# Adaptive-norm parameters from transposed weights on VectorE, half a block at a time

## The chip, the cores and the metric

One core of a Trainium2 chip. The metric is the device time in microseconds of one execution; the time before is the median of three runs. TensorE (PE) does the matrix products, PEld is its weight load, VectorE (DVE), ScalarE (ACT) and GpSimd (POOL) the elementwise work, SyncE (SP) issues most loads.

## The reference, cut to what matters

Two layers of a trunk over 512 tokens of width 1024, with 256 context tokens. Layer 0 mixes by attention, layer 1 by a convolution module; behind each stands an expert mixer with product keys. Every sub-layer is modulated by parameters that come from the conditioning vector `c` alone:

```python
def ada_params(cond, w, b):
    return jnp.split(jax.nn.silu(cond) @ w + b, 6, axis=-1)
...
for l in range(DEPTH):
    sh1, sc1, g1, sh2, sc2, g2 = ada_params(c, w_ada[l], b_ada[l])     # w_ada[l]: 1024 x 6144
    a_lat = modulate(rms_norm(h_lat, g_norm1[l]), sh1, sc1)            # x * (1 + scale) + shift
    ...
    h_lat = h_lat + g1[:, None, :] * y_lat
    h_lat = h_lat + g2[:, None, :] * peer_ffn(modulate(rms_norm(h_lat, g_norm2[l]), sh2, sc2), *peer_p)
```

For each layer that is one vector of 1024 times a matrix of 1024 x 6144. In `peer_ffn` each token has 8 heads with 2 key halves; from 128 keys of each half the best 16 are taken, and the best 16 of their sums name the experts whose rows of two tables (16384 x 1024) act on the token.

## The kernel before

The 6144 columns of a layer's parameters are cut into 48 blocks of 128: blocks 0 to 7 are sh1, 8 to 15 sc1, 16 to 23 g1, 24 to 31 sh2, 32 to 39 sc2, 40 to 47 g2. Shifts and scales are wanted as columns (one parameter on each partition, `par`, [128, 48]), the two gates as rows on all partitions (read back from a [128, 1024] tensor in DRAM, `g1d` and `g2d`). A block of weights is [128, 8, 128], 512 KB in pieces of 512 bytes. Each stage computes the blocks in its own way:

- Start: blocks 0 to 15 of layer 0 are products on PE (L985).
- Projections of the attention (span 41 to 235 us): layer 0's blocks 16 to 23, by a `stepper` with method "v". Eight products with a column of the conditioning vector are added up on DVE (L752, L754), a ones-matmul on PE sums over the partitions (`bcast`, L893) and DVE adds the bias (L894).
- Attention (235 to 505 us): layer 0's blocks 24 to 39, method "g". POOL does products and sums (L765 to L768), PE transposes the result (L886), DVE sums it (L888) and adds the bias (L889).
- Front of the first mixer: layer 1's blocks 6 to 19 on PE (`on_pe`: a gate by L807, a column by L805, 8 products each), one in each of the 16 head halves and a second in the first two. The loop over the halves (`hp`) multiplies the tokens with 512 KB of query weights in three passes (L142 to L144), copies the result on ACT and scores it against the keys (L257); DVE takes the best 16 (`top16`, L215; L219 is its maximum). DVE and ACT then prepare the first expert rows (u_hi L169, u_lo L173).
- Side step of the first mixer: layer 1's blocks 20 to 23 on PE (L807) while the gate matrix is built (`gbuild`).
- First expert loop: layer 0's blocks 40 to 47 and layer 1's 0 to 5 and 24 to 39, 30 blocks, by `slow`, three iterations for a block. DVE adds up four products in the first, four in the second (L852, L854); in the third PE does the ones-matmul (L869, L872) into PSUM columns that the scores leave free, and the next block's load is issued into the one buffer. DVE adds the bias an iteration later.
- Front of the second mixer: layer 1's blocks 40 to 47 on PE (L807), in the first half of the head halves.

The expert loop goes over 128 chunks of 128 experts. An iteration scores a chunk of `u` (three passes, `s1`), loads a later chunk of `v` (`load_v`, L558) and of `u` (L164), splits the next `v` into a high and a low part (`prep`: v_hi on ACT L579, v_lo on DVE L581), accumulates on PE (`s2`, L602, 18 products) and does two or three steps of the fourth token tile, whose experts' rows are gathered one by one (`fetch` on POOL L613, `gather_step` on DVE L621, L625). For the first 97 iterations `u` and the ada step are part of it.

Engines take their instructions in the order in which the code emits them, and that order is written out by hand; a load on SP's queue waits for its buffer, and what is emitted later on SP waits behind it. The lines of the loop that set it:

```python
    for m in range(NCHUNK):
        ...
        load_v(m + 4 if tail else m + 2 if m + 2 < busy else m + 3)
        while pdone < min(m + 1 + tail, NCHUNK - 1):
            pdone += 1
            prep(pdone, c + 1 if c + 1 < NCHUNK else None)
        ...
        while gdone < goal:
            gather_step(gdone)
            gdone += 1
        if beside is not None and c < NCHUNK:
            try:
                beside.send(room)
```

Of the kernel before, what the change touches and what calls it, by code (L numbers as in the profile page):

```python
# [23 lines left out]
D = 1024  # L24
KD = 8
# [14 lines left out]
B0, B1, B2, B3, FRONT_TWICE = 8, 6, 20, 40, (0, 1)  # L40

# [3 lines left out]
HOW = "vga"  # L45
# [101 lines left out]
def peer(k, h, xr, h_done, A, sh, g2d, wq, sk, uT, un, vn, out_open, out_cb, side=None, front=None, slow=None):  # L147
# [116 lines left out]
    front_step = front and front(qp, lambda: psf.tile([128, TT, 128], F32, name="gp", bufs=4))  # L264
    for hp in range(16):
# [47 lines left out]
    while front_step is not None and front_step():  # L313
        pass
# [164 lines left out]
    side_step = side and side(gp, lambda: psf.tile([128, TT, 128], F32, name="scp", bufs=2))  # L479

# [32 lines left out]
    for b in range(nb):  # L513
# [15 lines left out]
        if side_step is not None:  # L529
            side_step()  # L530
    while side_step is not None and side_step():
        pass
# [126 lines left out]
    beside = slow(bs) if slow is not None else None  # L659
    if beside is not None:  # L660
        next(beside)
# [4 lines left out]
    for m in range(NCHUNK):  # L666
# [8 lines left out]
        if c < NCHUNK:  # L675
            room = s1p[c][:, NTD:T]
            s1_gelu(c)
# [22 lines left out]
        if beside is not None and c < NCHUNK:  # L700
            try:
                beside.send(room)
            except StopIteration:
                beside = None
        if m == busy:
            nc.sync.dma_start(hres, hd)
            nc.sync.dma_start(hg, g2d)
# [26 lines left out]
class Ada:  # L734
# [3 lines left out]
    def __init__(self, k, l, cond, w, bT, brow):  # L738
        self.k, self.l, self.cond, self.w, self.bT, self.brow = k, l, cond, w, bT, brow
        self.par = k.const.tile([128, 48], F32, name="ada_par%d" % l)  # L740

    def load(self, pool, f0, bufs):
        t = pool.tile([128, KD, 128], F32, name="ada_w", bufs=bufs)
        self.k.nc.sync.dma_start(t, self.w[:, f0:f0 + 128].rearrange("(kk p) f -> p kk f", p=128))
        return t

    def partial(self, how, t, acc):

        nc = self.k.nc
        c = self.cond  # L750
        if how == "v":
            nc.vector.tensor_scalar(acc, t[:, 0, :], c[:, 0:1], None, op0=OP.mult)  # L752
            for kk in range(1, KD):
                nc.vector.scalar_tensor_tensor(acc, t[:, kk, :], c[:, kk:kk + 1], acc, op0=OP.mult, op1=OP.add)  # L754
            return
        g = nc.gpsimd
        for kk in range(KD):
            if how == "a" or (how == "m" and kk % 2):
                nc.scalar.activation(t[:, kk, :], t[:, kk, :], AF.Copy, scale=c[:, kk:kk + 1])
        if how == "m":  # L760
            t2 = t.rearrange("p (k two) f -> p k two f", two=2)[:, :, 0, :]
            g.tensor_tensor(t2, t2, c.rearrange("p (k two) -> p k two", two=2)[:, :, 0:1].to_broadcast([128, 4, 128]),
                            op=OP.mult)
        if how == "g":
            g.tensor_tensor(t, t, c[:, :, None].to_broadcast([128, KD, 128]), op=OP.mult)  # L765
        g.tensor_tensor(t[:, 0:4, :], t[:, 0:4, :], t[:, 4:8, :], op=OP.add)
        g.tensor_tensor(t[:, 0:2, :], t[:, 0:2, :], t[:, 2:4, :], op=OP.add)
        g.tensor_tensor(acc, t[:, 0, :], t[:, 1, :], op=OP.add)  # L768

    def stepper(self, pool, psum, blocks, eng, g1_dst, g2_dst, lag=1, wbufs=2):  # L770

        nc = self.k.nc
        todo, loaded, accs, stores = list(blocks), [], [], []

        def reduce(f, acc):
            p = psum()
            if f // 8 in (2, 5):
                o = f % 8 * 128
                br = pool.tile([128, 128], F32, name="ada_br", bufs=lag)
                nc.sync.dma_start(br, row_bcast(self.brow[f * 128:(f + 1) * 128], 128))  # L780
                self.bcast(p[:, 0, :], acc[:, 0, :], br, br)
                stores.append(((g1_dst if f < 24 else g2_dst)[:, o:o + 128], br))
            else:
                self.columns(p, acc, f, 1)

        summed = []

        def on_pe():

            if stores:  # L790
                nc.sync.dma_start(*stores.pop(0))
            if summed:
                f, p, br = summed.pop(0)
                if br is None:
                    nc.vector.tensor_tensor(self.par[:, f:f + 1], p[:, 0, 0:1], self.bT[:, f:f + 1], op=OP.add)
                else:
                    nc.vector.tensor_tensor(br, p[:, 0, :], br, op=OP.add)
                    o = f % 8 * 128
                    stores.append(((g1_dst if f < 24 else g2_dst)[:, o:o + 128], br))
# [17 lines left out]
        if eng == "p":  # L817
            return on_pe
# [17 lines left out]
    def slow(self, pool, blocks, dst=None):  # L836
# [20 lines left out]
        for n, f in enumerate(blocks):  # L857
            acc = pool.tile([128, 128], F32, name="ada_acc", bufs=2)
            if after:
                after.pop(0)()  # L860
# [1166 lines left out]
```

## Time and profile before

| | us |
|---|---|
| median of 3 runs | 3362.16 (3361.88 to 3362.23) |
| profiled execution, its own time | 3360.77 |
| its span | 3359.0 |
| PE busy | 3206.8 (95%) |
| DVE busy | 2578.6 (77%) |
| ACT busy | 1283.1 (38%) |
| POOL busy | 1009.9 (30%) |

The span is the time from the first to the last instruction of one profiled execution. Busy times of an engine are sums over its instructions. The chain of waits goes back from the last instruction, at each step to what released it. A row of the chain or of a timeline has its start and its length in us; x counts the instructions in it, and brackets hold the idle time before it and what ended that.

### The profile page before, as it was taken

The numbers are of one execution on the slowest core, as the hardware profiler recorded it, in microseconds if no ns is written. First come the engines' busy times: TensorE is split into PE (matmuls) and PEld (weight loads), VectorE is DVE, ScalarE is ACT, GpSimd is POOL, SyncE is SP. The second block draws the span as 40 slices with busy tenths as digits, with TensorE's granted clock in tenths as the row PEclk, the third lists the DMA queues.
The fourth block names the chain that finished last, engine by engine and source line by source line (L and its number), as shares of the span: only waits on it lengthen the run. The fifth ranks groups of instructions, "written<-read, shape, count | busy, mean of one in ns | idle before, by whom it ended". The sixth has DMA issues, their size and how long they took to land.

```text
span 3359.0 us, 45727 instructions
## 1 busy us (share of the span) xinstructions
PE 3206.8 (95%) x16982; PEld 2779.5 (83%) x16982; DVE 2578.6 (77%) x4720; ACT 1283.1 (38%) x2060; POOL 1009.9 (30%) x816
## 2 busy tenths in 40 slices
PE   8899999978999999999998998988999999999998
PEld 5775568978999999999986867878999999999986
DVE  3657746889688888888888976999767777777787
ACT  3435533345433333333335224335433333333332
POOL 1347413300133333333342002320033333333343
PEclk9989999989999999999999999999999999999999
DMA  6412125346899999999894113326788888898896
GB/s 198 129 49 75 57 82 162 104 174 249 279 318 325 326 320 320 327 322 319 310 333 142 51 44 119 114 96 237 263 291 302 302 309 302 303 307 302 307 320 210
DMA packets 373678, 764.33 MB, mean 228 GB/s; under 512 B 24144, under 2 KB 221008, under 8 KB 366160
## 3 DMA queue, kind: packets, MB, share of 16 engines
q1 hardware_dynamic: 292816, 442.62, 38.6%
q0 software_dynamic: 73728, 268.47, 23.1%
q10 hardware_dynamic: 6912, 50.33, 3.7%
q8 instruction: 133, 2.18, 0.3%
q14 instruction: 89, 0.73, 0.1%
HBM read 702.61 MB, written 58.72 MB: 227 GB/s over the span
## 4 chain that ended last, share of the span: by engine, by line
PE 79%; DVE 12%; issue 4%; ACT 2%; DMA 2%; SPq 1%; POOL 0%; ACTq 0%; DVEq 0%; POOLq 0%
PE acc L602 26%; PE s L142 11%; PE s L143 11%; PE s L144 11%; DVE eij L453 3%; PE y L1622 2%; PE cz L142 2%; PE cz L144 2%; PE cz L143 2%; PE z L144 1%; PE z L142 1%; PE z L143 1%; DVE ahl L455 1%; PE ot L1407 1%; DVE u_lo L173 1%
## 5 line engine op out<-in xcount | busy, mean ns | idle before, releaser
L143 PE MATMUL s<-hhi,u_lo 128*128 128x384 f32 (+1 forms) x2304 | 790.0, 343 | 14.8 <-DVE u_lo L173 14.6
L142 PE MATMUL s<-hhi,u_hi 128*128 128x384 f32 (+1 forms) x2304 | 798.1, 346 | 3.0 <-ACT u_hi L169 3.0
L144 PE MATMUL s<-hlo,u_hi 128*128 128x384 f32 (+1 forms) x2304 | 789.6, 343 | 0.0
L613 POOL DMA_INDIRECT row<-in_u_dram,eidx x256 | 317.8, 1242 | 997.0 <-DVE row L621 499.2
L613 POOL DMA_INDIRECT row<-in_v_dram,eidx x256 | 355.8, 1390 | 535.2 <-DVE gacc L625 477.1
L581 DVE TENSOR_TENSOR v_lo<-v_raw,v_hi 128x1024 fp32r<-128x1024 f32 x192 | 235.2, 1225 | 318.8 <-ACT v_hi L579 317.8
L579 ACT ACTIVATE v_hi<-v_raw 128x1024 fp32r<-128x1024 f32 x192 | 203.8, 1062 | 681.2 <-PE acc L602 669.2
L143 PEld LDWEIGHTS s<-hhi,u_lo 128*128 128x128 f32 x2304 | 435.6, 189 | 33.4 <-DVE u_lo L173 17.8
L142 PEld LDWEIGHTS s<-hhi,u_hi 128*128 128x128 f32 x2304 | 435.6, 189 | 18.9 <-ACT u_hi L169 3.7
L144 PEld LDWEIGHTS s<-hlo,u_hi 128*128 128x128 f32 x2304 | 434.7, 189 | 10.2
L602 PE MATMUL acc<-v_hi,w_hi 128*128 128x512 f32 x1344 | 418.1, 392 | 4.2 <-ACT w_hi L590 4.2
L602 PE MATMUL acc<-v_hi,w_lo 128*128 128x512 f32 x1344 | 416.3, 391 | 0.0
L602 PE MATMUL acc<-v_lo,w_hi 128*128 128x512 f32 x1344 | 416.1, 391 | 0.0
L173 DVE TENSOR_TENSOR u_lo<-u_raw,u_hi 128x1024 fp32r<-128x1024 f32 x242 | 295.1, 1219 | 47.9 <-ACT u_hi L169 47.9
L625 DVE SCALAR_TENSOR_TENSOR gacc<-row,gwgt,gacc 128x1024 f32<-128x1024 f32 x254 | 325.5, 1281 | 4.3
L169 ACT ACTIVATE u_hi<-u_raw 128x1024 fp32r<-128x1024 f32 x288 | 302.1, 1049 | 14.9 <-ACT stg L472 10.1
L621 DVE SCALAR_TENSOR_TENSOR row<-row,hg 128x1024 f32<-128x1024 f32 x256 | 301.0, 1220 | 0.0
L602 PEld LDWEIGHTS acc<-v_lo,w_hi 128*128 128x128 f32 x1344 | 252.3, 188 | 56.0
L602 PEld LDWEIGHTS acc<-v_hi,w_lo 128*128 128x128 f32 x1344 | 252.2, 188 | 54.6
L602 PEld LDWEIGHTS acc<-v_hi,w_hi 128*128 128x128 f32 x1344 | 249.2, 188 | 46.0 <-ACT w_hi L590 6.5
L590 ACT ACTIVATE w_hi<-w_f 128x384 fp32r<-128x384 f32 x256 | 134.7, 526 | 332.9 <-DVE w_f L588 316.1
L310 ACT ACTIVATE ring<-s 128x384 f32<-128x384 f32 x256 | 125.8, 491 | 322.1 <-PE s L144 322.1
(445 smaller groups left out, 4938.3 us busy)
## 6 DMA issues: line engine op xcount, KB each, us to landing
u_raw<-in_uT_dram SPq DMA_DIRECT2D x256, 512.0 KB, 5.9
v_raw<-in_v_dram SPq DMA_DIRECT2D x192, 512.0 KB, 5.9
Gd<-stg ACTq DMA_DIRECT2D x48, 1024.0 KB, 4.4
g_in<-Gd SPq DMA_DIRECT2D x128, 384.0 KB, 6.9
ada_w<-in_w_ada_dram SPq DMA_DIRECT2D x80, 512.0 KB, 5.6
u_raw<-in_v_dram SPq DMA_DIRECT2D x64, 512.0 KB, 5.1
u_raw<-in_wq_dram SPq DMA_DIRECT2D x32, 512.0 KB, 4.7
ada_w<-in_w_ada_dram SPq DMA_DIRECT2D x8, 1024.0 KB, 12.0
```

The costliest lines, as they stand in the source:

```text
L142: nc.tensor.matmul(out, lhsT=lh, rhs=rh, start=first, stop=False)
L143: nc.tensor.matmul(out, lhsT=ll, rhs=rh, start=False, stop=False)
L144: nc.tensor.matmul(out, lhsT=lh, rhs=rl, start=False, stop=last)
L169: nc.scalar.activation(uh, u, AF.Copy)
L173: lo_eng.tensor_tensor(ul, u, uh.bitcast(F32), op=OP.subtract)
L579: nc.scalar.activation(vh, v, AF.Copy)
L581: nc.vector.tensor_tensor(vl, v, vh.bitcast(F32), op=OP.subtract)
L590: nc.scalar.activation(wh, w, AF.Copy)
L602: nc.tensor.matmul(acc[tt][hf], lhsT=w[:, s], rhs=v[:, hf * 512:(hf + 1) * 512], start=f and n == 0, stop=l and n == 2)
L613: nc.gpsimd.indirect_dma_start(out=r, out_offset=None, in_=un if n < 128 else vn, in_offset=bass.IndirectOffsetOnAxis(ap=eidx[:, c:c + 1], ...
L621: nc.vector.scalar_tensor_tensor(r, r, 1.0, hg, op0=OP.mult, op1=OP.mult, accum_out=act[:, c:c + 1])
L625: nc.vector.scalar_tensor_tensor(gacc, r, wgt[:, c:c + 1], gacc, op0=OP.mult, op1=OP.add)
```

## The change

The ada weights come transposed, [6144, 1024], so that a block's 128 parameters lie on the partitions and the 1024 summands on the free axis. A half block is one load of 256 KB ([128 x 512], 2 KB a row) and one DVE instruction: multiply with silu(c), which stands as a row on all partitions (`crow`), and sum along the row into a column of `par` (first half) or `half` (second half). Once in 8 blocks the halves and the bias are added, and a gate group is stored to DRAM as [8, 128] and later read back as a row on all partitions (`gate_row`). The next half's load is emitted right behind the multiply that frees its buffer.

Where: layer 0's blocks 16 to 23 in the projections and 24 to 39 in the attention (two buffers, two halves at a step); layer 0's 40 to 47 and layer 1's 0 to 39 in the first expert loop (one buffer, one half in an iteration, 96 halves); layer 1's 40 to 47 in the second expert loop (one half in every fourth iteration). Blocks 0 to 15 of layer 0 stay on PE at the start. The fronts, the side step and their arguments of `peer` go, and so does POOL's work on ada. `crow` is made at the start: a broadcast load, a sigmoid on ACT and a multiply on DVE. The modulation of the second mixer is emitted before the convolution, not after it.

```diff
-    def load(self, pool, f0, bufs):
...
-    def stepper(self, pool, psum, blocks, eng, g1_dst, g2_dst, lag=1, wbufs=2):
...
-    def slow(self, pool, blocks, dst=None):
...
+    def blocks(self, pool, blocks, bufs, pause=0):
+
+        nc, todo, loaded = self.k.nc, [(f, i) for f in blocks for i in range(2)], []
+
+        def load():
             if todo:
...
+                f, i = todo.pop(0)
+                t = pool.tile([128, D // 2], F32, name="ada_w", bufs=bufs)
+                nc.sync.dma_start(t, self.wT[f * 128:(f + 1) * 128, i * 512:(i + 1) * 512])
+                loaded.append((f, i, t))
+        for _ in range(bufs):
+            load()
+        yield
+        while loaded:
+            f, i, t = loaded.pop(0)
+            nc.vector.scalar_tensor_tensor(t, t, 1.0, self.k.crow[:, i * 512:(i + 1) * 512], op0=OP.mult, op1=OP.mult,
+                                           accum_out=self.half[:, f % 8:f % 8 + 1] if i else self.par[:, f:f + 1])
+            if f % 8 == 7 and i:
+                o = slice(f - 7, f + 1)
+                nc.vector.tensor_tensor(self.half, self.half, self.bT[:, o], op=OP.add)
+                nc.vector.tensor_tensor(self.par[:, o], self.par[:, o], self.half, op=OP.add)
+                if f // 8 in self.gate:
+                    nc.sync.dma_start(self.gate[f // 8].rearrange("f p -> p f"), self.par[:, o])
+            load()
+            for _ in range(1 + pause):
+                yield
+
+def gate_row(g):
+    return g.rearrange("f p -> (f p)").partition_broadcast(128)
...
-        if front_step is not None:
-            front_step()
-            if hp in FRONT_TWICE:
-                front_step()
...
-        if side_step is not None:
-            side_step()
...
-        if beside is not None and c < NCHUNK:
-            try:
-                beside.send(room)
-            except StopIteration:
-                beside = None
+        next(beside, None)
...
+    nc.sync.dma_start(cr, row_bcast(a["crow"], D))
...
+    S.activation(k.crow, cr, AF.Sigmoid)
+    V.tensor_tensor(k.crow, cr, k.crow, op=OP.mult)
     Am = [modulation(k, pp, vecs["g1T"], par[:, s], 8, "Am%d" % s) for s in range(2)]
...
+    gate_blocks = ada.blocks(adp, range(16, 24), 2)
...
+    next_blocks = ada.blocks(adp, range(24, 40), 2)
...
+        def beside0(pool):
+            yield from ada0.blocks(pool, range(40, 48), 1)
+            yield from ada1.blocks(pool, range(40), 1)
+
+        def beside1(pool):
+            yield from ada1.blocks(pool, range(40, 48), 1, 3)
```

## Rows read from the trace of the kernel before

**Rows 1.** The page, part 4: shares of the chain that ended last.
```profile
PE 79%; DVE 12%; issue 4%; ACT 2%; DMA 2%; SPq 1%; POOL 0%; ACTq 0%; DVEq 0%; POOLq 0%
```
**Rows 2.** Expert loops by windows: us; PE, PEld, DVE, ACT, POOL busy; PEclk, DMA.
```profile
875.00:1671.00 796.00, 795.68 (x4051) 724.62 (x4051) 669.71 (x1019) 289.11 (x384) 289.86 (x227) 1.00 0.91 320
2419.00:3209.00 790.00, 789.84 (x3994) 719.08 (x3994) 590.04 (x750) 289.93 (x385) 290.27 (x227) 1.00 0.88 301
```
**Rows 3.** Chain in the first front: a gate block and a column block.
```profile
541.28 1.78 PE gp L807 x16
...
549.44 1.68 PE gp L805 x16
```
**Rows 4.** Chain in the second front: two successive heads' scores without ada.
```profile
2142.33 0.89 PE scp L257 x8
...
2148.68 0.89 PE scp L257 x8
```
**Rows 5.** Timeline of DVE: search in the first front, first u_lo of both mixers.
```profile
625.98 0.88 DVE L219 MAX8 S1v<-sc 128x8 f32<-128x128 f32 x4 [2.69 <-ACT sc L260]
...
639.42 0.85 DVE L219 MAX8 S1v<-sc 128x8 f32<-128x128 f32 x4
...
676.05 1.22 DVE L173 TENSOR_TENSOR u_lo<-u_raw,u_hi 128x1024 fp32r<-128x1024 f32 x1 [8.38 <-ACT u_hi L169]
...
2226.10 1.22 DVE L173 TENSOR_TENSOR u_lo<-u_raw,u_hi 128x1024 fp32r<-128x1024 f32 x1 [4.55 <-ACT u_hi L169]
```
**Rows 6.** Timeline of PE, then chain: accumulating products in both expert loops.
```profile
875.07 0.74 PE L602 MATMUL acc<-v_hi,w_hi 128*128 128x512 f32 x2
...
896.67 0.22 PE s L872 x2
...
1662.97 4.12 PE acc L602 x18
...
2419.29 4.38 PE acc L602 x18
...
3200.37 4.12 PE acc L602 x18
```
**Rows 7.** DVE multiplies by tile: ns min/median/max, first and last start.
```profile
L621 DVE SCALAR_TENSOR_TENSOR row<-row,hg x114: 1210/1220/1225, 959.9 to 1346.1; 128x1024 f32<-128x1024 f32 x114
...
L854 DVE SCALAR_TENSOR_TENSOR ada_acc<-ada_w,cond,ada_acc x210: 343/352/419, 883.1 to 1643.1; 128x128 f32<-128x128 f32 x105
```
**Rows 8.** First loop: SP's and ACT's timeline, us to landing of two v loads.
```profile
1216.02 0.38 SPq L744 DMA_DIRECT2D ada_w<-in_w_ada_dram  x1
...
1217.37 0.34 SPq L558 DMA_DIRECT2D v_raw<-in_v_dram  x1
...
v_raw<-in_v_dram SPq DMA_DIRECT2D x1, 512.0 KB, 8.0
...
v_raw<-in_v_dram SPq DMA_DIRECT2D x1, 512.0 KB, 9.7
...
1223.33 1.06 ACT L579 ACTIVATE v_hi<-v_raw 128x1024 fp32r<-128x1024 f32 x1 [3.68 <-PE acc L602]
```
**Rows 9.** Projections: PE's timeline, a window of low granted clock, the ones-matmuls.
```profile
146.96 0.80 PE L144 MATMUL z<-w_lo,aTl 128*128 128x512 f32 x1 [4.81 <-DVE w_lo L1029]
...
169.16 0.80 PE L144 MATMUL z<-w_lo,aE 128*128 128x512 f32 x1 [5.97 <-DVE w_lo L1029]
...
169.00:176.00 7.00, 6.84 (x18) 5.38 (x19) 1.84 (x3) 0.00 (x0) 1.04 (x1) 0.55 0.17 52
...
L893 PE MATMUL tp<-ada_acc,ones 128*128 128x128 f32 x16 | 3.3, 287 | 4.2 <-DVE ada_acc L754 3.9 <-ACT t L1166 0.3
```
**Rows 10.** Attention: DVE sums (busy, mean; then min/median/max), and PE's idle.
```profile
L889 DVE TENSOR_TENSOR ada_par<-ada_par,vec 128x1 f32<-128x1 f32 x16 | 16.5, 1030 | 0.6
...
L889 DVE TENSOR_TENSOR ada_par<-ada_par,vec x16: 158/1534/1999, 260.2 to 399.5; 128x1 f32<-128x1 f32 x16
...
397.31 0.90 PE L1392 MATMUL pt<-ident,Pr 128*128 128x128 f32 x3 [2.25 <-DVE kT L1341]
```

More of the change, by code (lines that the diff above doesn't have):

```diff
@@ L44 @@
 GPART = 4
-HOW = "vga"
 ADA_KV = (3,)
@@ L144, in matmul3, with peer @@
     nc.tensor.matmul(out, lhsT=lh, rhs=rl, start=False, stop=last)
-def peer(k, h, xr, h_done, A, sh, g2d, wq, sk, uT, un, vn, out_open, out_cb, side=None, front=None, slow=None):
+def peer(k, h, xr, h_done, A, sh, g2d, wq, sk, uT, un, vn, out_open, out_cb, slow=None):
     nc = k.nc
@@ L658, in peer @@
     pdone = 0
-    beside = slow(bs) if slow is not None else None
-    if beside is not None:
-        next(beside)
+    beside = slow(bs)
     dec = decode_last()
@@ L747, in partial @@
[L747 to L768, printed above, removed]
@@ L882, in columns @@
-    def columns(self, p, acc, f, n):
-        nc = self.k.nc
-        for i in range(n):
-            nc.tensor.transpose(p[:, i, :], acc[:, i, :], self.k.ident)
-        o = self.par[:, f:f + n]
-        nc.vector.tensor_reduce(o, p[:, 0:n, :], axis=AX.X, op=OP.add)
-        nc.vector.tensor_tensor(o, o, self.bT[:, f:f + n], op=OP.add)
-    def bcast(self, p, acc, dst, brow):
-        nc = self.k.nc
-        nc.tensor.matmul(p, lhsT=self.k.ones, rhs=acc, start=True, stop=True)
-        nc.vector.tensor_tensor(dst, p, brow, op=OP.add)
+        self.half = k.const.tile([128, 8], F32, name="ada_half%d" % l)
@@ L1103, in attention, with ada_step @@
     r1 = lst.enter_context(k.pool("a_r1"))
-    ada_step = ada.stepper(adp, lambda: psz.tile([128, 4, 128], F32, name="tp", bufs=2), range(16, 16 + B0), HOW[0], k.g1d[0], None)
+    gate_blocks = ada.blocks(adp, range(16, 24), 2)
+    def ada_step():
+        next(gate_blocks, True)
+        return next(gate_blocks, True)
     qn = r1.tile([128, 4, 8, 64], F32, name="qn")
@@ L1307, in attention @@
     q_half(1)
-    while ada_step():
+    while ada_step() is None:
         pass
@@ L1494, in attention @@
     g1b = hA.tile([128, D], F32, name="g1b")
-    nc.sync.dma_start(g1b, k.g1d[0])
-    ada_ps = lambda: psh.tile([128, 4, 128], F32, name="pt", bufs=3)
-    steps = [ada.stepper(adp, ada_ps, range(16 + B0, 40), HOW[1], None, None)]
+    nc.sync.dma_start(g1b, gate_row(ada.gate[2]))
+    next_blocks = ada.blocks(adp, range(24, 40), 2)
     def ada_step():
-        if steps and not steps[0]():
-            steps.pop(0)
-        return steps
+        next(next_blocks, True)
+        return next(next_blocks, True)
     units = [(kind, hd, m) for kind in "nm" for hd in range(8) for m in range(4)]
@@ L1546, in attention @@
         due.pop()()
-    while ada_step():
+    while ada_step() is None:
         pass
@@ L1692, in conv @@
     ns.close()
-    nc.sync.dma_start(g1b, k.g1d[1])
+    nc.sync.dma_start(g1b, gate_row(ada.gate[2]))
     nc.sync.dma_start(b2b, row_bcast(a["b_pw2"], D))
@@ L1894, in trunk @@
         hs = ExitStack()
-        ada0 = Ada(k, 0, None, a["w_ada0"], None, a["b_ada0"])
-        ada1 = Ada(k, 1, None, a["w_ada1"], None, a["b_ada1"])
+        ada0, ada1 = (Ada(k, l, a["wT_ada%d" % l]) for l in range(2))
         R = dict(side="right")
@@ L1937, in store @@
             nc.sync.dma_start(out[tt * 128:(tt + 1) * 128, d], y[:, d])
-        peer(k, h, xr, hn.close, A2, ada1.par[:, 24:32], k.g2d[1], a["wq1"], a["sk1"], a["uT1"], a["u1"], a["v1"],
-             None, store, None, front(range(B3, 48)))
+        peer(k, h, xr, hn.close, A2, ada1.par[:, 24:32], ada1.gate[5], a["wq1"], a["sk1"], a["uT1"], a["u1"], a["v1"],
+             None, store, beside1)
 def layout(inp):
```

138 lines of the change are left out of this document (14 added, 124 removed).

## The prediction

> **What bounds the kernel now.** I read the chain of waits first: TensorE (PE) is 79% of it, VectorE (DVE) 12% [rows 1]. So time saved on PE counts, and time saved elsewhere only where PE stands still for it. The windows by stage say the same of the two expert loops: PE is busy in 795.68 of 796 us in the first and 789.84 of 790 in the second, while DVE has 126 and 200 us to spare [rows 2]. I then took the places where the adaptive-norm parameters ("ada" below) are computed, one after another, and looked in each for PE work of ada and for PE idle that ada's work ends.
>
> **The change part by part.**
>
> Fronts. In the query projections ahead of the first mixer, PE computes 4 gate blocks at 1.78 us and 10 column blocks at 1.68 [rows 3]: 7.1 + 16.8 = 23.9 us. In the second front it computes 8 gate blocks: 14.2. All of it goes. Does the time go with it? PE needs 6.35 us for a head half without ada, as the later heads of the second front show (2142.33 to 2148.68) [rows 4], 12.70 for a pair. DVE's top-16 search needs 13.44 us for a pair (625.98 to 639.42) [rows 5]. So DVE falls behind by 0.74 a pair, 5.9 us over 8 pairs. At the end of the first front DVE now waits 8.38 us for ACT before its first u_lo [rows 5]; 5.9 fits in. Before the second it waits 4.55, and there half the heads already ran without ada: a lag of 3.8 where I would compute 3.0. At that rate 16 heads cost 7.6 of the 8.38. The margin is thin, 0.8 to 2.5 us, but it holds, so I take all 38.1.
>
> Gate matrix. From the first u_lo to the first accumulating matmul of the loop it is 199.0 us in the first mixer (676.05 to 875.07) and 193.2 in the second (2226.10 to 2419.29) [rows 5, 6]. The first alone has the side step with four gate blocks on PE. That goes: 5.8.
>
> First expert loop, PE. Each of the 30 blocks sends a ones-matmul of 0.22 us: 6.6. Against the second loop, which has none, the same stretch is 787.9 to 781.1 (875.07 to 1662.97, 2419.29 to 3200.37) [rows 6], 6.8 longer. I take 6.8.
>
> First expert loop, DVE. A 128x1024 multiply-and-sum takes 1.22 us and a 128x128 product 0.352 [rows 7]; between them by columns a 128x512 takes 0.72, with its sum some 0.8 (an estimate). 96 of these are 77 us; removed are 30 x 8 x 0.352 = 84. DVE's load stays where it is, under a PE that is busy throughout. The loads become 96 of 256 KB for 30 of 512 KB; 66 more issues at 0.38 us [rows 8] are 25 us of SP's 796. They cost nothing by themselves. Their place in SP's queue is the main risk (first rival).
>
> Second expert loop. It gains 16 multiplies, 13 us of DVE, one in every fourth iteration: 0, covered by the 200 us of DVE idle under a busy PE [rows 2].
>
> Projection. PE stands still 4.81, 5.97 and 3.90 us at three places, each ended by DVE that had been held in a block's eight ada products: 14.7 us [rows 9]. A step is now two multiplies, so about 1 us each should remain: 11.7 back. The 16 ones-matmuls of 3.3 us go too [rows 9], 15.0 in all. After such an idle the granted clock was 0.55 for 7 us [rows 9], 3 us lost, some 8 over the three places; without the idle part of it returns. I take 2, with 0 and 8 as ends.
>
> Attention. POOL's products go, and with them PE's transposes and 16 sums on DVE of 1.03 us mean, 0.158 at best [rows 10]: 16.5 us of DVE for 32 multiplies of 0.8, 26. PE idle ended by kT behind such sums is 2.25 us at 397.31, and 8.1 in seven such places [rows 10]. The new work on DVE is longer by 9 us, but split finer, so I take half, 4. Ends: +8, and -10, if each of the 32 multiplies held PE up for 0.3.
>
> Small edits. Ahead of the first norm, ScalarE gets a 128x1024 sigmoid (1.06 by the v_hi row [rows 8]) and DVE a 128x1024 multiply (1.22 [rows 7]), both before the modulation that PE's first products wait for: 2.3 with no overlap. Behind them comes a 512 KB broadcast load. I take -2, ends 0 and -5. The modulation of the second mixer moves ahead of the convolution, some short DVE operations that leave the second front's start: 0, at most 2 gained. Gates now go out as four stores of 4-byte elements and come back as broadcast loads. No row shows such a store. Each is followed by many iterations or units before its row is read, so 0; the bound is a few us at one place, the attention's output gate.
>
> Sum: 23.9 + 14.2 + 5.8 + 6.8 + 15.0 + 2 + 4 - 2 = 69.7. The profiled execution took 3360.8 us, so 3291.1; it stands 1.4 under the median of the runs, so 3292.5. I say **3292**.
>
> **The rivals.**
>
> SP's queue in the first expert loop. Now an ada load is issued in every third iteration. After the change every iteration ends with a multiply, the last thing DVE does in it, and one buffer serves all halves, so SP stands there until DVE is done. Behind it in SP's queue are the next iteration's loads of u and v; both are then issued about one iteration ahead of use instead of two. The loop that this closes: X from the issue of ada until v has landed, 1.06 for ScalarE's v_hi [rows 8], then DVE's work of an iteration, 669.71 / 96 = 6.98 [rows 2], over two iterations: 2P >= X + 8.04. PE's own period is 8.31 (781.1 over 94 iterations [rows 6]), so it decides from X = 8.6 on. Today's burst gives X = 1217.37 - 1216.02 + 8.0 = 9.35 [rows 8], with 512 KB of ada in 512-byte pieces ahead; the new load is half as many bytes, 1.25 MB for 1.5 in the burst, so 7.8 by bytes. I expect 8 to 9 (an estimate), and PE's buffers ahead take up single late ones. The mild case is X as today: P = 8.70, 96 x 0.39 = 37 us, 3330 at its end and 3315 on the way. The strong case is the way to slower: the slowest landing today is 9.7, X = 11.05, P = 9.55, 96 x 1.24 = 119, **3411**. It decides from X = 10.0 (P = 9.03), where the whole 69.7 is eaten. For it speaks that the wait comes three times as often and that the ada bytes of the loop grow from 15.7 to 25.2 MB, 12 GB/s on top of 320 at a DMA share of 0.91 [rows 2]; against it the smaller single load in longer pieces.
>
> DVE becomes the bound of both fronts. The margin above is 0.8 to 2.5 us on 125. If search, evacuations and POOL's splits disturb each other by another 0.3 us a head, 5 us are lost in each front: 3302. Against it stands that the two fronts' waits, 8.38 and 4.55, fit the lag.
>
> The multiplies wait for POOL. The sum L889 shows that a short DVE operation beside POOL can take 1.534 us (median) for 0.158 [rows 10]. If half of the 48 multiplies of projection and attention wait 1.4 us, DVE loses 34 us; the 16 sums lost 14 and left PE 8.1 idle, so at that rate 20 us: 3312. The Trainium skill ("SBUF — State Buffer", section "Who interferes with whom") states that a DVE instruction with two inputs in SBUF contends with a GpSimd instruction that reads SBUF, and that the loser blocks for the whole instruction; the new multiply has two such inputs. The trace's 0.158 and 1.534 us agree with that, and by the rule the time would be this rival's 3312. Against the rival: POOL's ada products, part of what the sums waited for, go away.
>
> **How the numbers follow.** Forecast 0.60; SP's queue mild 0.15, near no change 0.02, strong 0.07; DVE bound in the fronts 0.09; waits for POOL 0.07. A measurement of this kernel can tell 0.2%, 6.7 us, from no change. Faster is then 0.60 + 0.15 + 0.09 + 0.07 = 0.91, same 0.02, slower 0.07. The forecast's own ends: clock (6 more), attention (4 more) and small edits (4 more) give 3278; attention at its worst 3306. The range takes 3 more below and above goes to the mild SP case: 3275 to 3330.
>
> **What would show it.** Right: period of the query projections 6.35 to 6.7 us from the first head on, and DVE's wait before its first u_lo near 1 to 3 us; first u_lo to first accumulating matmul 193; the first loop's stretch 781 to 782, as the second's, with no ACT v_hi ended by v's landing; PE idle at the three places of the projection 1 us each. Wrong: PE idle in the first loop that goes back through v_hi to a load of v (rival one); PE or ACT waiting for the top-16 search at the end of a front (rival two); multiplies of 1.5 us and more beside POOL (rival three). The forecast falls if the first loop's period is above 8.6, or if the fronts shrink by under 30 of 38.

## The result, and the profile after

The changed kernel took 3418.28 us (median of 4 runs, 3415.34 to 3421.57) against 3362.19 of the kernel before in runs beside it: a ratio of 1.0165 (1.0148 to 1.0183), 56 us slower. The forecast was 3292. The span went from 3359.0 to 3419.8 us (the profiled execution of the changed kernel is the slowest of its four), and that difference is best read stage by stage. The borders are the first instructions of a kind in the two timelines; the middle column is the prediction's term.

| stage | forecast, us | measured, us |
|---|---|---|
| start to the first projection | +2 | +2.2 (47.1 to 49.3) |
| projections to the first scores | -17 | -16.9 (187.9 to 171.0) |
| attention to the first query projection | -4 | **+11.6** (283.3 to 294.9) |
| first front to the first u_lo | -23.9 | -25.0 (157.7 to 132.7) |
| gate matrix of the first mixer | -5.8 | -5.2 (199.0 to 193.8) |
| first loop, 94 iterations | -6.8 | **+88.2** (787.7 to 876.0) |
| rest of the first loop | 0 | **+12.9** (146.4 to 159.3) |
| convolution and second front to u_lo | -14.2 | -15.8 (416.9 to 401.1) |
| gate matrix of the second mixer | 0 | +0.1 |
| second loop, 94 iterations | 0 | **+7.4** (780.9 to 788.3) |
| rest of the second loop | 0 | +1.3 |
| sum | -69.7 | +60.8 |

The gains forecast for the start, the projections, the fronts and the gate matrices came, each within 2 us. The loss is in four other places: the attention, the first loop, what follows it, and the second loop. The shares of the chain of waits (the page, part 4) show what kind of loss it is; [rows 1] had PE at 79% and DMA at 2%:

```profile
PE 53%; DVE 17%; DMA 17%; issue 7%; ACT 4%; SPq 2%; POOL 0%; ACTq 0%; DVEq 0%; POOLq 0%
```

The windows of the two loops, from the first accumulating product to the one 94 iterations later, answer to [rows 2] (us; busy time of PE, PEld, DVE, ACT, POOL with instructions; PEclk, DMA share, GB/s):

```profile
841.73:1717.69 875.96, 815.70 (x3948) 729.56 (x3949) 637.65 (x933) 276.60 (x379) 311.34 (x224) 0.97 0.84 294
2471.38:3259.66 788.28, 783.78 (x3948) 713.17 (x3949) 591.83 (x776) 286.51 (x380) 299.37 (x224) 1.00 0.86 304
```

In the first, PE stands still for 60 us, while DMA is less busy than before (0.84 for 0.91) and DVE is idle for 238 us. PE is also busy for 815.70 us, where the same products take 780.92 when nothing stops them (below, "Both loops mended"): some 35 us more, at a granted clock of 0.97 for 1.00. Together that is the 95 us by which the loop exceeds 781. They are not spread evenly: by the starts of the accumulating products, 32 of the 94 iterations are longer than 8.6 us, and the other 62 take 8.3 or 8.4. So neither a full DMA nor a full DVE seems to make this loop slow; something waits in turn. The waits of the loop (engine, line, what ended the wait; us in all, times, longest) name it; the first row is the kernel before, the others the changed one:

```profile
ACT v_hi L579 <- PE acc L602: 332.8, 91, 4.0
...
ACT v_hi L563 <- DMA v_raw<-in_v_dram: 478.0, 89, 16.1
...
SPq L729 <- DVE ada_w L736: 619.6, 81, 12.8
```

Before, v_hi waited for PE; now it waits for the load of v. The chain of waits inside the loop shows a ring: SP's ada load, the load of v behind it, v_hi, DVE's work down to the ada multiply, and an ada load again, two iterations on.

```profile
1304.62 0.33 SPq L729
...
1306.52 8.36 DMA v_raw<-in_v_dram
...
1314.98 1.07 ACT v_hi L563
...
1322.81 0.62 DVE ada_w L736 x2
...
1323.45 0.33 SPq L729
...
1324.36 9.02 DMA v_raw<-in_v_dram
```

From one ada load to the next in the ring it is 18.83 us (1304.62 to 1323.45) for two iterations, 9.4 for one; PE needs 8.31. X of the prediction, from ada's issue to v's landing, is 10.26 here (1306.52 + 8.36 - 1304.62), and from v's landing to the end of the multiply it is 8.6.

The fronts were as predicted. In the chain, two scores of the first front stand 6.35 us apart (8.13 with a column block in the kernel before, 551.12 to 559.25), and DVE's waits before its first u_lo are 3.23 us in both mixers, where [rows 5] had 8.38 and 4.55:

```profile
564.55 0.89 PE scp L254 x8
...
570.90 0.89 PE scp L254 x8
```
```profile
647.95 1.23 DVE L170 TENSOR_TENSOR u_lo<-u_raw,u_hi 128x1024 fp32r<-128x1024 f32 x1 [3.23 <-ACT u_hi L166]
...
2278.11 1.23 DVE L170 TENSOR_TENSOR u_lo<-u_raw,u_hi 128x1024 fp32r<-128x1024 f32 x1 [3.23 <-ACT u_hi L166]
```

In the projections, one of the three stops of [rows 9] is left (PE's timeline):

```profile
148.78 0.79 PE L141 MATMUL z<-w_lo,aTl 128*128 128x512 f32 x1 [4.37 <-DVE w_lo L888]
```

DVE's timeline just ahead of it has two multiplies of 1.71 and 1.51 us, where most take 0.69, and a split of 2.05, where one took 1.22 in the kernel before (145.69). POOL's products run beside them (POOL's timeline: the last row, and one of 1.84 us from 142.92):

```profile
143.60 1.71 DVE L736 SCALAR_TENSOR_TENSOR ada_w<-ada_w,crow 128x512 f32<-128x512 f32 x1
...
145.23 1.51 DVE L736 SCALAR_TENSOR_TENSOR ada_w<-ada_w,crow 128x512 f32<-128x512 f32 x1
...
146.68 2.05 DVE L888 TENSOR_TENSOR w_lo<-w_raw,w_hi 128x1024 fp32r<-128x1024 f32 x1
```
```profile
144.72 2.93 POOL L1001 TENSOR_TENSOR t<-kn 128x512 f32<-128x512 f32 x2
```

In the attention, PE now stops at each ada step of the neighbourhood heads (PE's timeline; three of six such rows), and DVE's timeline shows why: two multiplies of 0.94 and 0.93 us lie between one unit's normalisation and the next unit's scores.

```profile
241.14 0.69 PE L1317 MATMUL pt<-ident,Pr 128*128 128x128 f32 x2 [2.99 <-DVE kT L1218]
...
256.30 0.70 PE L1284 MATMUL sc<-kT,qT 64*128 64x256 f32 x2 [1.58 <-ACT Pr L1297]
...
270.26 0.44 PE L1317 MATMUL pt<-ident,Pr 128*128 128x128 f32 x2 [1.69 <-DVE kT L1218]
```
```profile
265.55 0.70 DVE L1304 TENSOR_SCALAR Pr<-Pr,z 128x448 f32<-128x448 f32 x1
266.16 0.94 DVE L736 SCALAR_TENSOR_TENSOR ada_w<-ada_w,crow 128x512 f32<-128x512 f32 x1
...
267.04 0.93 DVE L736 SCALAR_TENSOR_TENSOR ada_w<-ada_w,crow 128x512 f32<-128x512 f32 x1
...
267.90 0.42 DVE L1292 TENSOR_TENSOR sc<-sc,nbias 128x256 f32<-128x256 f32 x1
```

### The profile page after: what moved, and what is told of

It reads as the page before. It is cut to its first block, busy times and chain, and to the rows that moved or that the text cites. A ratio compares the mean times of both kernels' runs of the same rounds, so it can differ in the third digit from the quotient of the medians.

```text
span 3419.8 us, 44470 instructions
## 1 busy us (share of the span) xinstructions
PE 3201.7 (94%) x16474; PEld 2750.8 (80%) x16474; DVE 2540.3 (74%) x4662; ACT 1273.5 (37%) x2061; POOL 981.0 (29%) x752
## 4 chain that ended last, share of the span: by engine, by line
PE 53%; DVE 17%; DMA 17%; issue 7%; ACT 4%; SPq 2%; POOL 0%; ACTq 0%; DVEq 0%; POOLq 0%
PE acc L586 14%; DMA v_raw<-in_v_dram 13%; PE s L140 7%; PE s L141 7%; PE s L139 7%; DVE eij L443 2%; PE y L1483 2%; DVE u_lo L170 2%; DVE gacc L609 2%; PE cz L139 2%; DVE row L605 2%; PE cz L141 2%; PE cz L140 2%; ACT v_hi L563 2%; PE z L141 1%
## 5 line engine op out<-in xcount | busy, mean ns | idle before, releaser
L140 PE MATMUL s<-hhi,u_lo 128*128 128x384 f32 (+1 forms) x2304 | 803.9, 349 | 54.4 <-DVE u_lo L170 54.4
L139 PE MATMUL s<-hhi,u_hi 128*128 128x384 f32 (+1 forms) x2304 | 807.0, 350 | 29.9 <-ACT u_hi L166 29.9
L141 PE MATMUL s<-hlo,u_hi 128*128 128x384 f32 (+1 forms) x2304 | 798.8, 347 | 0.0
L597 POOL DMA_INDIRECT row<-in_u_dram,eidx x256 | 348.9, 1363 | 1004.4 <-DVE row L605 513.4
L597 POOL DMA_INDIRECT row<-in_v_dram,eidx x256 | 363.3, 1419 | 594.0 <-DVE gacc L609 534.0
L140 PEld LDWEIGHTS s<-hhi,u_lo 128*128 128x128 f32 x2304 | 442.7, 192 | 83.4 <-DVE u_lo L170 67.5
L139 PEld LDWEIGHTS s<-hhi,u_hi 128*128 128x128 f32 x2304 | 443.1, 192 | 55.2 <-ACT u_hi L166 39.6
L141 PEld LDWEIGHTS s<-hlo,u_hi 128*128 128x128 f32 x2304 | 442.3, 192 | 10.0
```

What stands on the lines that cost most here:

```text
L139: nc.tensor.matmul(out, lhsT=lh, rhs=rh, start=first, stop=False)
L140: nc.tensor.matmul(out, lhsT=ll, rhs=rh, start=False, stop=False)
L141: nc.tensor.matmul(out, lhsT=lh, rhs=rl, start=False, stop=last)
L597: nc.gpsimd.indirect_dma_start(out=r, out_offset=None, in_=un if n < 128 else vn, in_offset=bass.IndirectOffsetOnAxis(ap=eidx[:, c:c + 1], ...
```

## The experiments

The slivers, the later store, the attention as before and the wait in every second iteration were each run once. Their argument rests on the stages of the trace and not on differences of a few us in the time.

### The ada load behind the loads of u and v

The strongest suspect was the place of one instruction in SP's queue. Its edit lets the generator stop between the multiply and the load, and resumes it in the next iteration right after `load_v`:

```diff
         load_v(m + 4 if tail else m + 2 if m + 2 < busy else m + 3)
+        if out_open is not None:
+            next(beside, None)
...
+            if late:
+                yield
             load()
...
```

> The changed kernel, but in the first expert loop the next half's load is emitted behind the next iteration's loads of u and v, in place of right behind the multiply. Loads, bytes, the one buffer and the multiplies stay. In the changed kernel the stretch from the first accumulating matmul to the one 94 iterations later takes 876.0 us (787.7 before), the rest of the loop 159.3 (146.4 before). Theory A (place in SP's queue: u and v stand behind SP's wait for the multiply): u and v are issued two iterations ahead again; the stretch falls to 781 to 800 (the two gate stores may keep some 7 us each), the rest to 146 to 149, the time to some 3305 to 3330. Theory B (the transfers: 25.2 MB of ada in place of 15.7 slow the landing of v): the same bytes move, so the stretch stays above 840 and the time above 3380. Theory C (DVE, the bound through its multiplies): stays above 860.

It took 3328.42 us, a ratio of 0.9903 (0.9875 to 0.9932) to the kernel before: 90 us less than the changed kernel, with the same loads, bytes and multiplies. The window of the loop; the waits in it, v_hi's and SP's; and v's time from issue to landing, in the kernel before and here:

```profile
840.62:1637.75 797.13, 786.70 (x3949) 715.64 (x3949) 643.53 (x940) 286.99 (x380) 316.97 (x224) 0.99 0.93 326
```
```profile
ACT v_hi L563 <- PE acc L586: 318.0, 87, 4.0
...
ACT v_hi L563 <- DMA v_raw<-in_v_dram: 27.8, 4, 11.8
...
SPq L731 <- DVE ada_w L738: 493.2, 89, 15.0
```
```profile
DMA to landing us min/median/max: 3.2/6.5/9.7
...
DMA to landing us min/median/max: 4.7/8.3/18.4
```

v_hi waits for PE again and, but for 4 times, no longer for v. SP still stands 493 us for the multiplies; what changed is that u and v are ahead of that wait. This is theory A. Theory B, that the transfers alone cost the time, falls with the landings: v lands later than in the kernel before (median 8.3 us, 6.5 there), DMA is busier (0.93 for 0.91), and nothing is lost by it, since v is asked for early enough. All iterations are back at 8.31 us but two, of 16.89 and 15.93, both at a gate's store. The rest of the first loop is 1.6 us over the kernel before, for 12.9 in the changed kernel.

### The same wait with few bytes

Each load brings 32 of the 512 columns into one buffer that is kept; most of the weights of these blocks are left out.

```diff
...
-                t = pool.tile([128, D // 2], F32, name="ada_w", bufs=bufs)
-                nc.sync.dma_start(t, self.wT[f * 128:(f + 1) * 128, i * 512:(i + 1) * 512])
+                t = one if sliver else pool.tile([128, D // 2], F32, name="ada_w", bufs=bufs)
+                w = 32 if sliver else 512
+                nc.sync.dma_start(t[:, 0:w], self.wT[f * 128:(f + 1) * 128, i * 512:i * 512 + w])
...
```

> The changed kernel, but each load of the first expert loop brings 32 of the 512 columns (16 KB in place of 256 KB) into one buffer that is kept; order, wait and multiply stay. It leaves out most of the weights of those 48 blocks, so their parameters are other numbers. Theory A: the wait on SP is still there in every iteration; what shortens is only the transfer ahead of u and v, 240 KB of some 1.25 MB, so X (from the ada load's issue to v's landing), about 10.2 us in the changed kernel's chain, falls to 8.2 to 9.5, the period by half of that, and the stretch of 876 to between 785 and 845. Theory B: the bytes were the cost, so the stretch is that of the second loop, 781 to 790. The lead of v tells them apart where the stretch doesn't: by A a v load is issued some 8 us before its use, as in the changed kernel, by B as well but it lands in under 6.

```profile
841.96:1671.15 829.19, 795.04 (x3948) 715.20 (x3949) 636.28 (x932) 276.11 (x379) 314.84 (x223) 0.99 0.82 283
```

And v's time to landing in the first loop, with the whole ada loads (the run of the next section, whose first loop has the same loads in the same places) and with the slivers:

```profile
DMA to landing us min/median/max: 5.3/9.3/17.2
...
DMA to landing us min/median/max: 4.9/8.5/16.3
```

The time was 3370.87 us. 829.2 us is inside theory A's range: with 1/16 of the bytes the loop is still 48 us above the 781 that PE needs. Two iterations at the gate stores (15.83 and 19.40 us) make 18.6 of that; the other 30 are the wait's, where the changed kernel has some 78 (876.0 less 781 and about 17 for its stores). v landed a median of 8.5 us after its issue, not under 6 as B would have it. So some 48 of the 78 us hang on ada's 256 KB going first, and the other 30 are there with almost no ada bytes at all.

### A gate's store one step later

```diff
                 if f // 8 in self.gate:
-                    nc.sync.dma_start(self.gate[f // 8].rearrange("f p -> p f"), self.par[:, o])
+                    store = self.gate[f // 8].rearrange("f p -> p f"), self.par[:, o]
...
+            if store is not None:
+                nc.sync.dma_start(*store)
+                store = None
```

> The changed kernel, but a gate's store is emitted one step of ada later (one iteration in the first loop, four in the second), when the sums that it reads are long done; it is the same store of 1024 elements of 4 bytes. In the second loop of the changed kernel one iteration of 94 takes 15.67 us in place of 8.31, at the store (2983.5). If SP's wait for the sums is the cause, that iteration falls to 8.3 and the stretch from 788.3 to 781; if the store itself holds up the loads behind it, the iteration moves four later and stays near 15; if both, 10 to 13. The first loop changes by under 10 us either way. Time 3405 to 3420.

The time was 3413.41 us. The second loop lost its long iteration, all 94 take 781 us (window), which is the expectation's first answer; the first loop stayed as long (879.0 us). But the store is no small thing (DMA issues, one window each: KB, us to landing):

```profile
2470.82:3251.78 780.96, 780.96 (x3948) 711.03 (x3949) 591.96 (x776) 286.63 (x380) 299.19 (x224) 1.00 0.87 307
```
```profile
gate<-ada_par SPq DMA_DIRECT2D x1, 4.0 KB, 12.7
...
v_raw<-in_v_dram SPq DMA_DIRECT2D x1, 512.0 KB, 12.1
```

4 KB took 12.7 us, and the next v, issued 7.5 us after the store, 12.1; v's median in that loop up to there is 7.5. What changed is that SP no longer stands at the store until DVE has the sums, so v goes out with its lead of two iterations, and 12 us fit in. So the wait decided. That the slow store makes the wait dearer is read from these rows; no run here has a quick store. The Trainium skill ("DMA: Bandwidth & Descriptors", section "Rules for kernel authors") states that a last dimension that isn't contiguous becomes one descriptor per element. The trace agrees: in the 13.2 us from the issue of this store of 1024 single elements 1126 packets are under 512 B, and 125 in a stretch as long 20 us earlier.

### The attention as before

Blocks 24 to 39 of layer 0 by POOL, PE and DVE, with the old weights (512 KB a block):

```diff
-    next_blocks = ada.blocks(adp, range(24, 40), 2)
+    step_g = ada.stepper(hp, lambda: psh.tile([128, 4, 128], F32, name="pt", bufs=3), range(24, 40), a["w_ada0"], k.cond[:, 0, :])
...
```

> The changed kernel, but blocks 24 to 39 of layer 0 are computed in the attention as before (products and sums on POOL, a transpose on PE, a sum and the bias on DVE). From the attention's first scores to the first query projection it is 294.9 us in the changed kernel (220.33 to 515.24) and 283.3 before. If the two multiplies of a step, 1.7 us between two softmaxes, are what makes PE stop (1.58 and 1.69 us at each step of the neighbourhood heads) and its granted clock fall (0.70 and 0.85), then 281 to 287 here, and the time is 8 to 14 us under the changed kernel's: some 3405. If the loss comes from something that entered the attention otherwise (the projections' end 15 us earlier, the broadcast load of the gate), it stays at 291 to 297.

The time was 3411.49 us. The attention took 284.3 us, 10.6 less than in the changed kernel, as the first of the two expected. The time fell by less, 6.8 us for the 8 to 14 expected: the first loop, which the edit doesn't touch, took 883.1 us here for 876.0 (879.0 with the later store), so a few us there say nothing. The attention's window, and those of the changed kernel (first) for the same stretch:

```profile
220.33:515.24 294.91, 273.41 (x1126) 168.91 (x1127) 179.08 (x354) 133.88 (x323) 68.12 (x81) 0.91 0.23 79
220.33:310.00 89.67, 79.86 (x296) 48.27 (x296) 59.71 (x129) 35.99 (x110) 38.81 (x59) 0.77 0.20 68
```
```profile
216.99:501.33 284.34, 267.01 (x1143) 167.87 (x1143) 183.46 (x318) 134.28 (x323) 140.78 (x145) 0.94 0.25 82
216.99:307.00 90.01, 86.74 (x375) 54.79 (x376) 70.94 (x149) 46.71 (x143) 72.66 (x92) 0.88 0.29 87
```

DVE is busier with the old way (183.5 us for 179.1), and yet PE is less idle and its granted clock is higher in the first 90 us (0.88 for 0.77). The sum of DVE's work is not what counts there.

### Both loops mended

The two edits of the loops together: the load moved in the first loop, the store later in both.

> The changed kernel with the ada load of the first expert loop behind the next iteration's loads of u and v, and each gate's store a step later than its sums, in both loops. No byte, multiply or store is less than in the changed kernel. With the load alone moved the stretch of the first loop was 797.1 us, of which two iterations at the gate stores took 16.89 and 15.93 in place of 8.31, and the second loop's was 786.6; with the store alone moved the second loop's was 781.0. If SP's waits for DVE are the whole loss of the loops, both stretches are 781 to 782 here, the rest of the first loop 146 to 148, and the time is 3328.4 - 16.2 - 5.6 = 3304 to 3309. If the ada bytes (12 GB/s more) cost something of their own, the first loop's stretch stays above 784.

3305.39 us, a ratio of 0.9835 (0.9818 to 0.9851). The windows of both loops:

```profile
840.70:1621.62 780.92, 780.92 (x3948) 711.03 (x3949) 643.62 (x940) 286.65 (x380) 318.34 (x224) 1.00 0.94 333
2362.92:3143.84 780.92, 780.92 (x3948) 711.03 (x3949) 591.97 (x776) 286.53 (x380) 298.15 (x224) 1.00 0.87 307
```

PE is never idle in either, at a DMA share of 0.94 in the first. The rest of the first loop is back at 147.5 us (159.3 in the changed kernel), so that loss was the same wait. In the chain of the changed kernel a load of v issued there at 1745.80, right behind those of the residual and of the gate's row, landed 13.46 us later.

### Three ways through the attention

On top of the mended loops: the attention as before; one multiply at twice as many places; all 32 multiplies in the second half, one for each unit. The last two edits:

```diff
-        next(next_blocks, True)
         return next(next_blocks, True)
...
-        if i % 4 == 0 if kind == "n" else i % 2 == 0:
+        if i % 2 == 0 if kind == "n" else True:
```
```diff
-        next(next_blocks, True)
         return next(next_blocks, True)
...
-        if i % 4 == 0 if kind == "n" else i % 2 == 0:
+        if kind == "m":
```

> As the kernel with both loops mended, and blocks 24 to 39 of layer 0 in the attention as before the change (POOL, PE, DVE). The attention alone undone went from 294.9 to 284.3 us. If the two gains add up, the time is 10 to 11 us under that of the loops mended: 3294 to 3298. If the loss in the attention only came and went with the loops' state, the two are equal.

> As the kernel with both loops mended, but in the attention one multiply at twice as many places instead of two at one. The multiplies, their bytes and POOL's work are the same. If what stops PE is the length of DVE's extra work between two softmaxes (1.7 us for two), the idle of PE at a step falls to under 0.8 us, the granted clock rises from 0.70 and 0.85 to some 0.9, and the attention takes 284 to 289 us in place of 294.8: time 3296 to 3301. If the sum of DVE's work counts, it stays within 2 us of 294.8.

> As the kernel with both loops mended, but all 32 multiplies of the attention lie in its second half (the latent heads), one for each unit, and none in the neighbourhood heads. In the changed kernel the steps of the second half leave PE idle 0.8 to 0.9 us at two places, those of the first half 1.6 to 1.7 at five and 3.0 at one, with the clock at 0.70 and 0.85 there. If the loss belongs to the first half, whose softmaxes have no room on DVE, the attention takes 279 to 286 us, and the time is 3291 to 3298. If DVE is as short in the second half, the loss moves there and the time stays at 3304 to 3309.

They took 3292.31 us (ratio 0.9796, 0.9779 to 0.9812), 3292.37 (0.9791, 0.9775 to 0.9808) and 3289.71 (0.9787, 0.9771 to 0.9803): all 13 to 16 us under the loops mended alone, not told apart from each other by the intervals, and each 1 to 4 us under its expected range. The windows of the attention, spread and then second half:

```profile
218.22:499.76 281.54, 266.62 (x1127) 167.16 (x1127) 175.37 (x353) 134.10 (x323) 67.66 (x81) 0.93 0.23 82
218.22:308.00 89.78, 84.83 (x351) 53.08 (x352) 63.21 (x153) 42.97 (x131) 38.03 (x61) 0.85 0.22 79
```
```profile
220.49:495.73 275.24, 263.54 (x1127) 165.34 (x1127) 181.73 (x353) 134.96 (x323) 65.78 (x81) 0.94 0.24 84
220.49:310.00 89.51, 86.88 (x370) 54.76 (x371) 64.75 (x135) 46.55 (x141) 35.99 (x61) 0.87 0.12 40
```

With the same 32 multiplies the attention takes 294.9 us two at a place, 281.5 one at a place and 275.2 with all in the second half (282.2 in the old way); the last two expectations were on the pessimistic side (284 to 289 and 279 to 286). PE's stops at the single steps of the first half are 0.72 to 1.19 us, where under 0.8 was expected. The attention loses by the length of DVE's work at one place, not by its amount. The 19.7 us of that stage between two at a place and the second half are not all kept: the time falls by 15.7 (3305.4 to 3289.7), and the stage of the convolution and the second front is 2.1 us longer.

### The row of silu(c) in a gap

On top of the second half: the sigmoid and the multiply of the start go between two copies for which ScalarE waits for PE.

```diff
         S.activation(rows[:, i * 256:(i + 1) * 256], p[0:2, 0:256], AF.Copy)
+        if i == 6:
+            S.activation(k.crow, cr, AF.Sigmoid)
+            V.tensor_tensor(k.crow, cr, k.crow, op=OP.mult)
```

> As the kernel with both loops mended and the attention's multiplies in its second half, and the sigmoid and the multiply that make the row of silu(c) are emitted between the copies of the seventh and the eighth piece of the start's products, where ScalarE waits 3.08 us for PE and DVE some 10. In the changed kernel the two take 1.04 and 1.22 us ahead of the modulation, and the first projection starts at 49.1 to 49.3 us (47.1 before). If the two are hidden there, it starts at 46.8 to 47.3 and the time falls by 2 us, to 3287 to 3289; if the row's load (it landed at 37.0, issued at 26.84) comes too late for that place, ScalarE's last copy waits and nothing is gained.

3287.05 us, a ratio of 0.9776 (0.9759 to 0.9792), the lowest time of all: 2.2% under the kernel before. The first projection started at 47.7 us, 1.4 earlier than in the run without the edit (49.1) but later than the 46.8 to 47.3 expected; the time is in its range (3287 to 3289). The two instructions are hidden, as ScalarE's timeline shows: its last copy still waits 2.13 us for PE.

```profile
37.60 0.37 ACT L855 ACTIVATE rows<-z 2x256 f32<-2x256 f32 x1 [3.08 <-PE z L854]
37.88 1.04 ACT L857 ACTIVATE crow<-cr 128x1024 f32<-128x1024 f32 x1
41.05 0.37 ACT L855 ACTIVATE rows<-z 2x256 f32<-2x256 f32 x1 [2.13 <-PE z L854]
```

The time alone (2.7 us) is inside the intervals of the two runs.

### The wait in every second iteration only

One question was left: does the loss need the wait in every iteration? Here only the second half of each block is multiplied, one in every second iteration; the first halves are left out.

```diff
...
-            yield from ada1.blocks(pool, range(40), 1)
+            yield from ada1.blocks(pool, range(40), 1, 1, half=True)
```

> The changed kernel, but in the first expert loop only the second half of each block is multiplied, one in every second iteration; the load stays right behind the multiply and SP's wait too. It leaves out the first half of the sums of 48 blocks. If the loss needs the wait in successive iterations (v's lead shrinks and the next wait keeps it short), the iterations without a wait let SP run ahead again: the stretch is 781 to 790 but for 7 to 9 us at each of two gate stores, some 797 to 806 in all. If each wait costs by itself (95 us over some 94 waits), half of the 88 us stays: 825 to 840.

It took 3379.83 us, and the stretch 842.7, 3 us above the range of the second answer and far from the first, which I had held. Without the two iterations at gate stores (16.42 and 20.97 us) some 41 us remain for about 40 waits: 1 us each on average, though all of it lies in 17 longer iterations. The window, SP's waits, and the landing of a v load issued at 1236.28:

```profile
841.39:1684.09 842.70, 800.59 (x3948) 721.37 (x3949) 606.75 (x842) 276.76 (x377) 308.87 (x224) 0.98 0.83 291
```
```profile
SPq L731 <- DVE ada_w L738: 565.8, 41, 23.1
```
```profile
v_raw<-in_v_dram SPq DMA_DIRECT2D x1, 512.0 KB, 14.7
```

Here SP waits 13.8 us a time, and then sends the loads of two iterations one right behind the other; the last v of such a bunch lands 14.7 us after its issue. So by these rows there is a second way to lose by the same wait: not a ring over successive iterations, but a bunch after each. With the wait in every fourth iteration (the second loop) nothing is lost outside of the store. Where between two and four the loss ends was not tried.

## Why the prediction was wrong

**The rival named for the slower side is what happened.** "SP's queue in the first expert loop", strong case: 3411 us with a chance of 0.07. The ring was the one described, and its price was near: 2P = X + 8.04 with X = 11.05 was 9.55 us an iteration; in the ring of the chain X was 10.3 and the rest 8.6, 9.4 an iteration, and over the whole loop the mean is 9.3, gate stores included. That the time, 3418, stands so close to 3411 is partly luck. That case put 119 us into the first loop, where 95 came; the rest came from places that are not in its sum, the attention (15.6 us worse than forecast), the rest of the first loop (12.9) and the second loop (7.4).

**The step that failed** is the estimate of X: "so 7.8 by bytes. I expect 8 to 9", and with it the 0 for the place in SP's queue. X is 10.2 over the loop: v's median of 9.3 us to landing, as the run with the later store has it, and the 0.9 between the issues of ada and of v. Bytes were the wrong ground: with 16 KB of ada in place of 256 the same rule gives 6.3 (an estimate: 9.35 for 1.5 MB), and the slivers' run had 8.5 + 0.9 = 9.4. Why v needs that long in the ring is not shown by a run; in the rows, u goes out half a us ahead of it (SP's timeline, 1323.88 and 1324.36). But a long X costs only because v's lead is gone, and there the reading of [rows 8] was at fault: the prediction took 1216.02 to 1217.37 for a burst that the kernel before stands for every third iteration without loss. Its neighbours in SP's timeline of the kernel before say something else:

```profile
1209.06 0.33 SPq L558 DMA_DIRECT2D v_raw<-in_v_dram  x1
...
1225.67 0.33 SPq L558 DMA_DIRECT2D v_raw<-in_v_dram  x1
```

With 1217.37 of [rows 8], v goes out every 8.31 us (1209.06, 1217.37, 1225.67): its pace is set by its own buffer, and the ada load's wait, over at 1216.02, ends before it. That is so because there the load was emitted an iteration after the products that free its buffer. The new code emits it right behind the multiply, so the same wait sits one iteration earlier in the queue and ends some 7 us after v could have gone. That "the wait comes three times as often" was the lesser point: with the load moved it comes as often, and nothing is lost. Only at the wrong place does the number count, some 41 us for half the waits and 78 for all.

**The small loads.** "Each is followed by many iterations or units before its row is read, so 0" for the gates' stores: nobody waited for the row, but the loads behind the store did, 8.6 and 7.6 us in the first loop (16.89 and 15.93 against 8.31) and 5.7 to 7.4 in the second. Asking who reads the result was half the question; who is queued behind was the other. The rest of the first loop, +12.9, stood nowhere in the sum: the wait of the last ada steps met the residual's load there, and with the ada load moved 1.6 of it is left.

**The attention** was forecast at -4 with ends of +8 and -10 of gain, and lost 11.6. The mean of L889 (1.03 us, [rows 10]) hid two halves: in the neighbourhood heads of the kernel before, four of the six sums took 0.16 us (at 270.83 and 281.87 for two), in the latent heads most took 1.53. The new steps put 1.74 us (266.16 to 267.90) into the first kind of place, where 0.4 had stood. The fix that put them all into the second half took 19.7 us off that stage (294.9 to 275.2).

**What held.** The fronts (23.9 and 14.2 forecast, 25.0 and 15.8 measured), the gate matrix (5.8; 5.2), the projections (17; 16.9: 10.7 us less of PE idle for 11.7, 6.3 less of PE busy for 5.3), the start (2; 2.2), and the multiply's price, estimated at 0.8 and measured at 0.69 and 0.08 for its sum (first row, the loop; second, the projections and the attention):

```profile
L736 DVE SCALAR_TENSOR_TENSOR ada_w<-ada_w,crow x96: 679/686/741, 857.0 to 1749.0; 128x512 f32<-128x512 f32 x96
...
L736 DVE SCALAR_TENSOR_TENSOR ada_w<-ada_w,crow x48: 678/686/1705, 72.3 to 392.4; 128x512 f32<-128x512 f32 x48
```

With both loops mended and the attention's multiplies spread the whole came to 3292.4, the forecast's number, and each of its stages stands within 2.5 us of its term (the attention gained 1.8 for 4). That is a kernel with the ada load, the stores and the attention's steps in other places, not the one forecast. The DVE bound in the fronts didn't come (3.23 us left).

**The rival of multiplies that wait for POOL** showed its sign too, at a smaller price. Of the 48 in the projections and the attention 35 take 0.69 us, nine 0.91 to 0.94 and four 1.51 to 1.71. DVE loses some 5.6 us by them, where the rival had 34. Two of the four stand ahead of the stop of 4.37 us at 148.78, where the prediction had 1: with the split behind them DVE took 2.7 us longer than by 0.69, 0.69 and 1.22. No run takes POOL's work away, so the cause is read from the timelines. The Trainium skill's rule that was weighed ("SBUF — State Buffer", section "Who interferes with whom") agrees with these rows and with the 0.94 and 0.93 us at 266.16; the median stays at 686 ns, as in the loop.

## What to carry to other kernels

When a load's buffer is freed by the last operation of an iteration, emit the load an iteration later, behind the loads that must go out early: on one in-order queue a wait costs what is queued behind it, whoever reads its own data. Before costing a new wait at nothing, read the pace of the loads behind it in the timeline and ask whether the wait would end before or after that pace. A piece of side work is costed at the place where it lands (how long is the pause between two steps of the chain there), not by the sum of its engine.

## What the runs showed that was not expected

- A store of 4 KB in 1024 single elements took 12.7 us to land, and the next 512 KB load of v 12.1, against a median of 7.5 us for v in the same loop up to there.
- The loop ran without any PE idle at a DMA share of 0.94 and 333 GB/s, above the 0.91 and 320 of [rows 2], while the slow loop had 0.84 and 294.
- In the attention, PE's stops cost about twice their length. With the multiplies in the second half, PE was busy 263.5 us for 273.4 with the same products, and idle 11.7 for 21.5: of the 19.7 us of that stage, 9.8 are stops and 9.9 products that ran slower, at a granted clock of 0.91 for 0.94 over the attention and 0.77 for 0.87 over its first 90 us.
